# Sparse attention by pairs of heads on halves of the tensor engine, gate products between its steps and z products between those of the state-space mixer

## The chip, the cores and the metric

The kernel runs on one core of a Trainium2 chip. The metric is the time of one execution on the device in microseconds (us), as the median over the runs. The engines are named PE (tensor engine; PEld is its loading of weights), DVE (vector engine), ACT (scalar engine), POOL and SP; each works through its own queue.

## The reference, cut to what matters

The reference is a chain of three transformer blocks over 512 tokens of 1024 features. Only the first block is touched. It runs three mixers on the same normalized input, gates two of them, and joins them in one product:

```
o_nsa = sparse attention: 8 heads of 64 features, 2 groups of keys and values,
        = g0 * attention to compressed keys + g1 * attention to selected blocks + g2 * attention in a window
        (at 512 tokens every block is selected and the window holds every key:
         both are plain causal attention, each with its own keys and values)
o_nsa = o_nsa * silu(gate columns of the input product)
y     = state-space mixer: 8 heads, chunks of 128 tokens
o_ssd = rmsnorm(y * silu(z)) * g_ssd_norm
o_mem = attention to 256 memory tokens, 4 heads of 128
o_mem = o_mem * silu(its gate columns)
x     = rmsnorm(x + [o_nsa, o_ssd, o_mem] @ w_out) * g_final
```

## The kernel before, in words

Activations lie feature-major, as tiles of 128 features by 512 tokens. A float32 product of the large matrices is made as three products of two-part operands (`mm3`, lines 119 to 121, on a `Pair` of a high and a low part). `weight` (from line 96) loads a weight tile through SP and cuts it into parts: the high part is a copy on ACT (line 106), the low part a subtraction on DVE (line 107). There are 12 buffers for parts of 512 columns and 3 for raw tiles. PSUM has 6 banks under the name `ps` (`bank`) and 2 under `pt` (`bank2`).

`linear` goes through the output tiles of a product one at a time. Its first `head` tiles can go k tile by k tile, for 256 tokens and then for the other 256; its last `tail` tiles end by halves too. `Fill` gives out a product in parts of two k tiles (six products), to be put between steps of other work; its `evac` runs behind the last part of a tile.

The first block (`block1`) first does the attention to the memory (`memory`), then the sparse attention (`Nsa.attend`), then the mixer (`ssd`), then the joining product with `w["out"]`. The outputs of the mixers are the twelve tiles `o`: 0 to 3 sparse attention, 4 to 7 mixer, 8 to 11 memory.

`attend` makes queries, keys and values by `linear`, then the compressed scores of all heads, and then goes through 64 units (pair of heads j, head e of the pair, query tile i, branch b). `front` computes a unit's scores: one product over 128 rows (line 206), where the key tile `kp[b, g, e]` is zero in the 64 rows of the other head, plus the causal mask as a product with the identity (line 207); then the maximum on DVE (209, 211), the Exp on ACT (213), and the scaling on DVE (1035, 1036). `back` transposes the probabilities block by block (`turn`, 221), copies them on ACT (223), and multiplies them with the values (1050) into 64 of 128 partitions of a bank; the compressed branch is one more product (1047). Scores are issued three units ahead of their use.

`ssd` makes its inputs by `linear`, then goes through four chunks. Between their steps it calls `fill.run(2)`, 22 parts in all, on the 32 parts of the eight gate products (their evacuation is `ev_g`, lines 912 to 915). What is left is run behind the loop; then the four z products come by `linear` with `ev_z` (1262 to 1264), and then the norm. The joining product takes the parts of all twelve tiles in order of k.

The instructions of an engine are put in order when the kernel is built, by a planner that knows which operands are ready when. In the trace products of a later stage stand among those of an earlier one, as the products of the mixer's inputs do in the last 8 us of the attention.

Of the kernel before, what the change touches and what calls it, by code (L numbers as in the profile page):

```python
# [27 lines left out]
class Pair:  # L28
    """A float32 tensor as two float32r parts whose sum is the tensor."""
# [8 lines left out]
class Core:  # L38
    def __init__(self, ctx, tc):
# [28 lines left out]
                                fill=-1e30, base=0, channel_multiplier=1)  # L68
        self.mean = self.const.tile([P, 1], F32, name="mean")
# [25 lines left out]
    def weight(self, ap):  # L95
        """Parts of a weight tile [P, n], n <= 1024, from DRAM: Pairs of up to 512 columns each."""
# [29 lines left out]
    def split(self, x, g=None, pool=None, tag="xg", into=None, sl=None):  # L126
        """The parts of x * g, g a column per partition."""
# [11 lines left out]

    def linear(self, w, kt, x, evac, head=0, tail=0, pre=None):  # L140
        """F-major product: w [m tiles, P, kt * P] in DRAM, x a Pair per k tile, evac(m, psum, columns).
        The first `head` tiles go k by k, for one half of the tokens and then for the other, so that they can
        start on the first x. The last `tail` tiles end with the first half of the tokens of all of them before
        the second. pre is the norm in front, to be finished behind its squares' products."""
# [4 lines left out]
        for ms in groups:  # L149
# [3 lines left out]
            def mm(m, k, sl):  # L153
# [4 lines left out]
                self.mm3(qs[m][:, sl], ws[m, k // 8][k % 8 // 4][:, o:o + P], x[k][:, sl], k == 0, k == kt - 1)  # L158

            if head and ms[0] == 0:  # L160
                for sl in HALVES:
                    for k in range(kt):
                        for m in ms:
                            mm(m, k, sl)
# [32 lines left out]
    def row_of(self, q, rows, p):  # L197
        """Row p of the tile `rows` on all partitions, into q."""
        self.nc.tensor.matmul(q, self.ident[:, p:p + 1].to_broadcast([P, P]), rows, start=True, stop=True)

    def causal_probs(self, pool, lhs, rhs, i, scale, tag, **kw):
        """exp(s - max) of scale * lhs.T @ rhs for query tile i, keys up to it; and the row sums."""
        nc = self.nc
        n = (i + 1) * P
# [11 lines left out]
    def turn(self, pool, src, n):  # L216
        """The n blocks of src [P, n * P], each transposed: [P, n, P]."""
# [4 lines left out]
        t = pool.tile([P, 4, P], F32, tag="turn", name=self.name("turn"), bufs=3)  # L222
# [3 lines left out]
    def log1p_exp_neg_abs(self, pool, a, tags):  # L226
        """ln(1 + exp(-|a|)) by the series of 2 atanh(u / (2 + u))."""
# [16 lines left out]
    def rsqrt(self, y, q, n, eps, sl=FULL, w=None):  # L244
        """1 / sqrt(q / n + eps) into y, both at columns sl."""
# [17 lines left out]
    def columns(self, row):  # L263
        """A row on all partitions [P, n * P] as token columns [P, n]."""
# [10 lines left out]
class Sums:  # L275
    """Sums over features of tiles that come whole, or by halves of the tokens, in whole [P, 512] tiles.
    `late` takes the last tile straight to the tensor engine; else total() is called for."""
# [6 lines left out]
    def add(self, s, sl):  # L284
        """True when the sum at columns sl is complete, in PSUM."""
# [29 lines left out]
class Norm:  # L315
    """1 / sqrt(mean of squares + eps) per token, as a row on all partitions."""
# [22 lines left out]
class HeadNorm:  # L339
    """1 / sqrt(mean of squares + eps) over each of n tiles of features, for many of them at a time."""  # L340
# [10 lines left out]
    def add(self, h, s):  # L351
        """s, the squares of tile h."""
# [6 lines left out]
    def finish(self, a, b):  # L359
        """Tiles a to b have all been squared."""  # L360
# [3 lines left out]
    def row(self, h):  # L364
        """The row of tile h on all partitions, in PSUM."""
# [7 lines left out]
class Fill:  # L373
    """F-major products given out in small parts, to stand between the steps of other work."""
# [24 lines left out]
    def run(self, n=1):  # L399
        """n parts of two k tiles each, or all of them with n None."""  # L400
# [11 lines left out]
class Pre:  # L412
    """RMS norm in front of a product: parts of x * g, and 1 / rms per token, applied behind it."""
# [22 lines left out]
def post(c, x, y, norm, g, then):  # L436
    """x + y * norm * g in place; `then` gets each tile's number and columns as they are done."""
# [9 lines left out]
def ffn3(c, x, pre, g_post, w_in, w_out, then):  # L447
    """x + rms(swiglu(pre(x)), g_post), x in place."""
# [35 lines left out]
def mlstm(c, x, pre, w_rows, w_v, w_o, w_out, b_i, b_f, head_g, g_post, then):  # L484
    """x + rms(mlstm_mixer(pre(x)), g_post), x in place."""
    nc, mm = c.nc, c.nc.tensor.matmul
    H, L, NC, DK = 4, 128, 4, 128
    with ExitStack() as st:
# [70 lines left out]
        def scores(h):  # L559
            """Weighted scores, queries and keys of head h, and the decays of its state."""  # L560
# [79 lines left out]
def shared_kv(c, pre, w_k, w_v, kd, vd, filler):  # L640
    """Keys, feature-major, and values, token-major, of rms(x) into DRAM."""
# [22 lines left out]
def diff_attention(c, x, pre, w_q, kd, vd, lam_vecs, subln, w_out, lam_init, g_post, then):  # L664
    """x + rms(diff_attention(pre(x)), g_post), x in place."""
    nc, mm = c.nc, c.nc.tensor.matmul
    H, DH = 8, 64
    with ExitStack() as st:
# [38 lines left out]
        def front(j, i):  # L707
            """The difference of the two softmaxes of query tile i."""
# [184 lines left out]
def block1(c, x, w, v, then):  # L893
# [5 lines left out]
    with ExitStack() as out:  # L899
# [18 lines left out]
        for m in range(8):  # L918
            fill.put(w["gates"][m], KD, pre.xg, lambda q, m=m: ev_g(m, q))
# [1029 lines left out]
```

## Time and profile before

| | us |
|---|---|
| median of 3 runs | 3599.95 (3599.71 to 3602.56) |
| span of the profiled execution | 3597.9 |
| PE busy | 3505.6 (97%) |
| PEld busy | 2924.1 (81%) |
| DVE busy | 2058.8 (57%) |
| ACT busy | 1529.4 (43%) |
| POOL busy | 490.8 (14%) |

The runs' time is that of the whole execution on the device, the span runs from the first to the last instruction of one execution under the profiler; the two differ by some 2 us here. A busy share is an average over stages. Matmuls are pipelined and the ends of their records are modelled, so the starts of records tell more than their durations. A plain float32 product is two records, a transposition one. The stages follow each other in the trace like this: sparse attention from its compressed scores, 176 to 305 us; the mixer's inputs to 352, its loop to 405, the rest of the gate products and the z products to 441, the joining product after that.

### The profile page before, as it was taken

What the parts mean: (1) busy time and instruction counts of PE and PEld (TensorE: products, weight loads), DVE (VectorE), ACT (ScalarE), POOL (GpSimd) and SP (SyncE); (2) the same over time, 40 slices, a digit from 0 to 9 for tenths busy, and PEclk for the clock granted to TensorE, in tenths of its full rate; (3) what the DMA queues carried; (4) which work ended last, traced back from release to release, by engine and by line L of the source; (5) the groups of instructions that cost most, each with busy time, mean ns of one, the idle gap of its engine ahead of it and who ended that gap; (6) DMA issues with size and microseconds to landing.
All of it is one profiled execution on the core that took longest, in us unless ns stands there. A gap on an engine that the chain in (4) does not pass through costs nothing. (4 is left out here: it accounts for less than half of the span.)

```text
span 3597.9 us, 48095 instructions
## 1 busy us (share of the span) xinstructions
PE 3505.6 (97%) x18182; PEld 2924.1 (81%) x18182; DVE 2058.8 (57%) x3871; ACT 1529.4 (43%) x2866; POOL 490.8 (14%) x517
## 2 busy tenths in 40 slices
PE   8999999999999999999999999998999999999997
PEld 6767788788788888888887888887888887888886
DVE  6667759995456354633384663439443438673337
ACT  5454544663434242533344543336433335443335
POOL 2100111230010001201110220113110111020112
PEclk9999999999999999999999999999999999999999
DMA  4401232112323333333322133222533223123331
GB/s 146 126 7 48 91 110 94 53 54 71 100 88 98 96 101 96 108 94 100 94 84 70 59 97 103 91 92 74 185 102 103 90 86 92 58 88 94 99 94 65
DMA packets 109712, 323.94 MB, mean 90 GB/s; under 512 B 12328, under 2 KB 28456, under 8 KB 109480
## 3 DMA queue, kind: packets, MB, share of 16 engines
q1 hardware_dynamic: 93648, 299.27, 26.8%
q10 hardware_dynamic: 15832, 21.60, 1.8%
q8 instruction: 143, 2.34, 0.3%
q14 instruction: 89, 0.73, 0.1%
HBM read 308.23 MB, written 12.58 MB: 89 GB/s over the span
## 5 line engine op out<-in xcount | busy, mean ns | idle before, releaser
L119 PE MATMUL ps<-x,hi 128*128 128x512 f32 (+1 forms) x3520 | 1280.9, 366 | 6.0 <-ACT x L136 5.3
L120 PE MATMUL ps<-x,hi 128*128 128x512 f32 (+1 forms) x3520 | 1270.5, 362 | 9.3 <-DVE x L137 8.6
L121 PE MATMUL ps<-x,lo 128*128 128x512 f32 (+1 forms) x3520 | 1265.5, 360 | 2.4 <-DVE lo L107 2.4
L106 ACT CAST hi<-raw 128x512 fp32r<-128x512 f32 (+1 forms) x1112 | 668.9, 612 | 1269.3 <-PE ps L120 1127.3
L107 DVE TENSOR_TENSOR lo<-raw,hi 128x512 fp32r<-128x512 f32 (+1 forms) x1112 | 783.8, 714 | 712.1 <-ACT hi L106 710.2
L120 PEld LDWEIGHTS ps<-x,hi 128*128 128x128 f32 x3520 | 665.8, 189 | 115.7 <-DVE x L137 16.5
L119 PEld LDWEIGHTS ps<-x,hi 128*128 128x128 f32 x3520 | 662.7, 189 | 108.7 <-ACT x L136 9.2
L121 PEld LDWEIGHTS ps<-x,lo 128*128 128x128 f32 x3520 | 665.0, 189 | 103.6 <-DVE lo L107 2.9
L119 PE MATMUL ps<-h,hi 128*128 128x512 f32 (+1 forms) x990 | 367.2, 371 | 0.0
L121 PE MATMUL ps<-h,lo 128*128 128x512 f32 (+1 forms) x990 | 364.4, 368 | 0.0
L120 PE MATMUL ps<-h,hi 128*128 128x512 f32 (+1 forms) x990 | 361.4, 365 | 0.0
L466 POOL TENSOR_TENSOR gt<-gt,gt 128x512 f32<-128x512 f32 x88 | 137.7, 1566 | 1088.9 <-DVE gt L465 941.1
L121 PEld LDWEIGHTS ps<-h,lo 128*128 128x128 f32 x990 | 185.7, 188 | 34.3
L120 PEld LDWEIGHTS ps<-h,hi 128*128 128x128 f32 x990 | 185.8, 188 | 33.4
L119 PEld LDWEIGHTS ps<-h,hi 128*128 128x128 f32 x990 | 186.0, 188 | 30.7
L296 POOL TENSOR_TENSOR sqa<-sqa,sq 128x256 f32<-128x256 f32 (+1 forms) x171 | 166.9, 976 | 303.6 <-ACT sq L326 296.5
L134 DVE TENSOR_TENSOR h<-gt,h 128x512 fp32r<-128x512 f32 x110 | 76.7, 700 | 148.9 <-ACT h L133 146.9
L133 ACT CAST h<-gt 128x512 fp32r<-128x512 f32 x110 | 68.1, 620 | 182.6 <-POOL gt L466 174.4
L465 DVE TENSOR_TENSOR gt<-ps,rbc 128x512 f32<-128x512 f32 x88 | 60.8, 691 | 119.5 <-PE ps L121 119.5
L137 DVE SCALAR_TENSOR_TENSOR x<-x,c,x 128x256 fp32r<-128x256 f32 (+1 forms) x144 | 98.2, 686 | 22.6 <-ACT x L136 22.6
L136 ACT ACTIVATE x<-x,c 128x256 fp32r<-128x256 f32 (+1 forms) x144 | 75.5, 529 | 72.0 <-DVE x L443 56.9
L460 DVE TENSOR_TENSOR gt<-ps,rbc 128x512 f32<-128x512 f32 x88 | 60.8, 690 | 78.6 <-PE ps L121 78.6
(626 smaller groups left out, 4007.1 us busy)
## 6 DMA issues: line engine op xcount, KB each, us to landing
raw<-fi SPq DMA_DIRECT2D x220, 512.0 KB, 3.5
raw<-fo SPq DMA_DIRECT2D x80, 512.0 KB, 3.5
raw<-fo SPq DMA_DIRECT2D x80, 192.0 KB, 2.3
raw<-out SPq DMA_DIRECT2D x16, 512.0 KB, 3.5
raw<-qf SPq DMA_DIRECT2D x16, 512.0 KB, 3.5
raw<-mz SPq DMA_DIRECT2D x16, 512.0 KB, 3.5
raw<-pg SPq DMA_DIRECT2D x16, 512.0 KB, 3.5
raw<-mr SPq DMA_DIRECT2D x9, 512.0 KB, 3.7
```

The source lines that it names most:

```text
L106: nc.scalar.copy(hi[:, :b], raw[:, a:a + b])
L107: nc.vector.tensor_tensor(lo[:, :b], raw[:, a:a + b], hi[:, :b].bitcast(F32), ALU.subtract)
L119: mm(out, lhs.hi, rhs.hi, start=start, stop=False)
L120: mm(out, lhs.hi, rhs.lo, start=False, stop=False)
L121: mm(out, lhs.lo, rhs.hi, start=False, stop=stop)
L133: nc.scalar.copy(hi, x)
L134: nc.vector.tensor_tensor(lo, x, hi.bitcast(F32), ALU.subtract)
L136: nc.scalar.mul(hi, x, g)
L137: nc.vector.scalar_tensor_tensor(lo, x, g, hi.bitcast(F32), ALU.mult, ALU.subtract)
L296: nc.gpsimd.tensor_tensor(self.acc[:, sl], self.part[h][:, sl], s[:, sl], ALU.add)
L460: nc.vector.tensor_tensor(t, q, pre.row, ALU.mult)
L466: nc.gpsimd.tensor_tensor(u, u, hold[0], ALU.mult)
```

## The change

Scores are made for both heads of a pair at once: the key tile holds the same keys in both halves of the rows, and each head's product contracts over its own 64 rows into a bank of its own, in blocks of up to 256 keys that alternate between the halves. The mask is made in the same way, from constants `id2` and `above2`. A unit is now a pair of heads and a query tile, with both branches: 16 units, one ahead. Their value products alternate between the halves of the output partitions. A unit calls `fill.run(1)` twice; the fill holds seven of the eight gate products. The eighth and the four z products are given out in the mixer's loop; the multiplication with z follows behind the loop. The joining product starts with a head of four tiles, in the order of k 0 to 3, 8 to 11, 4 to 7.

```diff
+        self.id2 = self.const.tile([P, 2, P], BF, name="id2")
+        self.above2 = self.const.tile([P, 2, P], BF, name="above2")
+        for src, dst in ((self.identb, self.id2), (self.above, self.above2)):
+            for r in range(2):
+                for h in range(2):
+                    nc.vector.tensor_copy(dst[64 * r:64 * r + 64, h], src[64 * h:64 * h + 64])
...
-    def linear(self, w, kt, x, evac, head=0, tail=0, pre=None):
+    def linear(self, w, kt, x, evac, head=0, tail=0, pre=None, order=None):
...
+            ks = order if first and order else range(kt)
...
-    def causal_probs(self, pool, lhs, rhs, i, scale, tag, **kw):
+    def pair_scores(self, lhs, rhs, i):
+        mm, n = self.nc.tensor.matmul, (i + 1) * P
+        qs, rows = [self.bank(), self.bank()], [slice(0, 64), slice(64, 128)]
+        for a in range(0, n, 256):
+            b = min(a + 256, n)
+            for q, r in zip(qs, rows):
+                mm(q[:, a:b], lhs[r, i * P:n], rhs[r, a:b], start=a == 0, stop=False)
+        for h in range(2):
+            for q, r in zip(qs, rows):
+                mm(q[:, i * P:n], self.id2[r, h], self.above2[r, h], start=False, stop=h == 1)
+        return qs
+
+    def probs(self, pool, q, n, scale, tag, **kw):
-        q = self.bank()
-        nc.tensor.matmul(q[:, 0:n], lhs, rhs[:, 0:n], start=True, stop=False)
-        nc.tensor.matmul(q[:, i * P:n], self.identb, self.above, start=False, stop=True)
...
-            nsa.attend(st, o, place)
...
+            fill = Fill(c)
+            gate = lambda m: fill.put(w["gates"][m], KD, pre.xg, lambda q: ev_g(m, q))
+            for m in (4, 5, 6, 7, 0, 1, 2):
+                gate(m)
+            nsa.attend(st, o, place, fill)
+            gate(3)
...
-        fill = Fill(c)
-        for m in range(8):
-            fill.put(w["gates"][m], KD, pre.xg, lambda q, m=m: ev_g(m, q))
...
-        c.linear(w["out"], 12, og, ev_o, tail=2)
+        c.linear(w["out"], 12, og, ev_o, head=4, tail=2, order=[0, 1, 2, 3, 8, 9, 10, 11, 4, 5, 6, 7])
...
-        kp = {(b, g, e): til(f"kp{b}{g}{e}", pool=ap) for b in range(2) for g in range(2) for e in range(2)}
-        for (b, g, e), t in kp.items():
-            nc.gpsimd.memset(t[64 * (1 - e):64 * (1 - e) + 64], 0.0)
+        kp = {(b, g): til(f"kp{b}{g}", pool=ap) for b in range(2) for g in range(2)}
...
-        def front(j, e, i, b):
+        def front(j, i):
+            n, ex = (i + 1) * P, {}
+            for b in range(2):
+                for e, q in enumerate(c.pair_scores(qT[j], kp[b, j // 2], i)):
+                    x, sm = c.probs(a2, q, n, SC, "e", bufs=8)
+                    rs = til("rs_", (P, 1), pool=a2, bufs=8)
+                    nc.vector.reciprocal(rs, sm)
+                    nc.vector.tensor_scalar(x[:, 0:n], x[:, 0:n], rs, gv[:, i, 2 * j + e, b + 1:b + 2], ALU.mult, ALU.mult)
+                    ex[b, e] = x
             return ex
...
-        def back(j, e, i, b, ex):
+        def back(j, i, ex):
+            g, n, pt = j // 2, (i + 1) * P, {}
+            if i == 0:
                 oq[0] = c.bank()
+            for b in range(2):
+                for e in range(2):
+                    pt[b, e] = c.turn(a2, ex[b, e], i + 1, bufs=6)
+                fill.run(1)
+            dst = [oq[0][64 * e:64 * e + 64, i * P:n] for e in range(2)]
+            for e in range(2):
+                mm(dst[e], vcp[:, 2 * j + e], pc[g][:, i * P:n], start=True, stop=False)
+            for b in range(2):
+                for t in range(i + 1):
+                    for e in range(2):
+                        mm(dst[e], vt[b][:, t, 64 * g:64 * g + 64], pt[b, e][:, t], start=False, stop=b == 1 and t == i)
...
+        units = [(j, i) for j in range(4) for i in range(4)]
+        ready = [front(*units[0])]
         for n, u in enumerate(units):
+            if n + 1 < len(units):
+                ready.append(front(*units[n + 1]))
             back(*u, ready.pop(0))
...
+        zs = [None] * 4
+
+        def ev_z(m, q):
+            zs[m] = til(f"z{m}")
+            nc.vector.tensor_tensor(zs[m], q, r, ALU.mult)
+            nc.scalar.activation(zs[m], zs[m], AF.Silu)
+
+        for m in range(4):
+            fill.put(w["z"][m], KD, pre.xg, lambda q, m=m: ev_z(m, q))
...
         fill.run(None)
         norm = Norm(c, 4)
...
+        for m in range(4):
+            nc.vector.tensor_tensor(o[m], o[m], zs[m], ALU.mult)
             norm.square(o[m])
-
-        c.linear(w["z"], KD, pre.xg, ev_z)
```

The attention of the third block (`diff_attention`), which called `causal_probs` too, makes the same products in place and then calls `probs`.

## Rows read from the trace of the kernel before

**Rows 1.** Windows: core, stretch, its length, busy time and count per engine, clock, DMA.

```profile
190.00:297.00 107.00, 106.38 (x669) 70.09 (x669) 64.77 (x241) 58.71 (x183) 0.00 (x0) 1.00 0.02 6
352.00:405.50 53.50, 53.38 (x344) 42.21 (x342) 44.19 (x108) 33.43 (x51) 6.47 (x5) 1.00 0.18 55
```

**Rows 2.** Tensor engine groups by form, 190 to 297 us: busy, mean ns, idle before.

```profile
L1050 PE MATMUL ps<-turn,vt 128*64 128x128 f32 x292 | 40.8, 280 | 0.3 <-ACT turn L223 0.2
...
L221 PE MATMUL pt<-ident,e 128*128 128x128 f32 x146 | 27.0, 287 | 0.2 <-ACT pc L1029 0.2
...
L206 PE MATMUL ps<-kp,q 128*128 128x512 f32 x28 | 14.5, 599 | 0.0
...
L1047 PE MATMUL ps<-pc,vcp 128*64 128x128 f32 x60 | 12.5, 290 | 0.0
```

**Rows 3.** Timeline, tensor engine: start, from first start to last end, trains of eight records.

```profile
198.74 1.09 PE L221 MATMUL pt<-ident,e 128*128 128x128 f32 x8
...
281.02 1.09 PE L1050 MATMUL ps<-turn,vt 128*64 128x128 f32 x8
...
356.40 0.66 PE L1225 MATMUL ps<-M,xdt 128*64 128x128 f32 x8
```

**Rows 4.** Timeline, tensor engine: score steps of four lengths, one after the other.

```profile
180.75 0.44 PE L206 MATMUL ps<-kp,q 128*128 128x128 f32 x2
181.03 0.22 PE L207 MATMUL ps<-above,identb 128*128 128x128 bf16 x1
181.09 0.65 PE L206 MATMUL ps<-kp,q 128*128 128x256 f32 x2
...
181.63 0.65 PE L206 MATMUL ps<-kp,q 128*128 128x256 f32 x2
...
186.02 0.86 PE L206 MATMUL ps<-kp,q 128*128 128x384 f32 x2
...
186.78 1.08 PE L206 MATMUL ps<-kp,q 128*128 128x512 f32 x2
...
187.75 1.08 PE L206 MATMUL ps<-kp,q 128*128 128x512 f32 x2
```

**Rows 5.** Timeline: the mixer's last products, the first splits, the mixer's norm.

```profile
401.64 0.40 PE L120 MATMUL ps<-x,hi 128*128 128x512 f32 x1
...
403.04 0.40 PE L120 MATMUL ps<-x,hi 128*128 128x512 f32 x1
...
405.10 0.38 PE L1227 MATMUL ps<-cx,sn 128*64 128x128 f32 x2
...
406.56 0.68 DVE L912 TENSOR_TENSOR gt<-ps,rbc 128x512 f32<-128x512 f32 x1
...
406.68 1.14 ACT L133 CAST s<-o 128x512 fp32r<-128x512 f32 x2
...
444.71 1.13 PE L301 MATMUL pt<-sq,ones 128*128 128x512 f32 x2
...
452.11 1.29 ACT L133 CAST x<-o 128x512 fp32r<-128x512 f32 x2 [1.31 <-DVE o L1269]
```

**Rows 6.** Scalar engine groups by line, 352 to 405.5 us.

```profile
L913 ACT ACT_TABLE_LOAD x5 | 6.4, 1283 | 0.1
...
L913 ACT ACTIVATE gt<-gt 128x512 f32<-128x512 f32 x5 | 3.2, 631 | 0.1
```

**Rows 7.** Timeline, tensor engine: products of 256 columns, the 1st and 25th of a run.

```profile
492.86 0.28 PE L119 MATMUL ps<-x,hi 128*128 128x256 f32 x1
...
495.74 0.29 PE L119 MATMUL ps<-s,hi 128*128 128x256 f32 x1
```

**Rows 8.** Timeline and windows (granted clock behind POOL): an idle, and the clock after it.

```profile
33.00 1.02 PE L269 MATMUL pt<-mean,rbc 128*128 128x1 f32 x4 [5.76 <-DVE rbc L254]
...
32.00:34.00 2.00, 1.00 (x5) 1.00 (x5) 2.00 (x2) 0.44 (x1) 1.92 (x2) 0.50 0.44 178
34.00:36.00 2.00, 2.00 (x6) 1.61 (x6) 1.34 (x3) 1.28 (x3) 0.06 (x1) 0.50 0.00 0
```

More of the change, by code (lines that the diff above doesn't have):

```diff
@@ L157, in mm @@
                 o = (k % 4) * P
-                self.mm3(qs[m][:, sl], ws[m, k // 8][k % 8 // 4][:, o:o + P], x[k][:, sl], k == 0, k == kt - 1)
-            if head and ms[0] == 0:
+                self.mm3(qs[m][:, sl], ws[m, k // 8][k % 8 // 4][:, o:o + P], x[k][:, sl], k == 0, k == ks[-1])
+            first = head and ms[0] == 0
+            ks = order if first and order else range(kt)
+            if first:
                 for sl in HALVES:
-                    for k in range(kt):
+                    for k in ks:
                         for m in ms:
@@ L214, in causal_probs, with turn @@
         return e, mx[:, 1:2]
-    def turn(self, pool, src, n):
+    def turn(self, pool, src, n, bufs=3):
         nc = self.nc
@@ L221, in turn @@
             nc.tensor.transpose(q[:, k * P:(k + 1) * P], src[:, k * P:(k + 1) * P], self.ident)
-        t = pool.tile([P, 4, P], F32, tag="turn", name=self.name("turn"), bufs=3)
+        t = pool.tile([P, 4, P], F32, tag="turn", name=self.name("turn"), bufs=bufs)
         nc.scalar.copy(t[:, 0:n], q[:, 0:n * P].rearrange("p (a b) -> p a b", b=P))
@@ L713, in front @@
             n = (i + 1) * P
-            es = [c.causal_probs(d2, qT[j][:, i * P:n], kv[j][0][b], i, 1.0, f"e{b}") for b in range(2)]
+            es = []
+            for b in range(2):
+                q = c.bank()
+                mm(q[:, 0:n], qT[j][:, i * P:n], kv[j][0][b][:, 0:n], start=True, stop=False)
+                mm(q[:, i * P:n], c.identb, c.above, start=False, stop=True)
+                es.append(c.probs(d2, q, n, 1.0, f"e{b}"))
             rs = til("rs", (P, 2), pool=d2)
@@ L905, in block1, with ev_g @@
                 memory(c, cst, pre, w, v, o, place, nsa)
-            nsa.attend(st, o, place)
-        op = out.enter_context(c.tc.tile_pool(name=c.name("o"), bufs=1))
-        r = pre.row
-        def ev_g(m, q):
-            t = c.t512("gt")
-            nc.vector.tensor_tensor(t, q, r, ALU.mult)
-            nc.scalar.activation(t, t, AF.Silu)
-            i = m if m < 4 else m + 4
-            nc.gpsimd.tensor_tensor(o[i], o[i], t, ALU.mult)
-        fill = Fill(c)
-        for m in range(8):
-            fill.put(w["gates"][m], KD, pre.xg, lambda q, m=m: ev_g(m, q))
+            r = pre.row
+            def ev_g(m, q):
+                t = c.t512("gt")
+                nc.vector.tensor_tensor(t, q, r, ALU.mult)
+                nc.scalar.activation(t, t, AF.Silu)
+                i = m if m < 4 else m + 4
+                nc.gpsimd.tensor_tensor(o[i], o[i], t, ALU.mult)
+            fill = Fill(c)
[4 more added lines that the diff above has]
+            gate(3)
+        op = out.enter_context(c.tc.tile_pool(name=c.name("o"), bufs=1))
         ssd(c, pre, r, w, v, o, op, fill)
@@ L970, in rope, with attend @@
         nc.gpsimd.tensor_tensor(dst, src, t, ALU.add)
-    def attend(self, st, o, place):
+    def attend(self, st, o, place, fill):
         c, nc, til, v = self.c, self.c.nc, self.til, self.v
@@ L1037, in front @@
             return ex
         oq = [None]
-        def back(j, e, i, b, ex):
-            h, g, n = 2 * j + e, j // 2, (i + 1) * P
-            if e + i + b == 0:
+        def back(j, i, ex):
+            g, n, pt = j // 2, (i + 1) * P, {}
+            if i == 0:
                 oq[0] = c.bank()
-            dst = oq[0][64 * e:64 * e + 64, i * P:n]
-            if b == 0:
-                mm(dst, vcp[:, h], pc[g][:, i * P:n], start=True, stop=False)
-            pt = c.turn(a2, ex, i + 1)
-            for t in range(i + 1):
-                mm(dst, vt[b][:, t, 64 * g:64 * g + 64], pt[:, t], start=False, stop=b == 1 and t == i)
-            if (e, i, b) == (1, 3, 1):
+            for b in range(2):
[5 more added lines that the diff above has]
+                mm(dst[e], vcp[:, 2 * j + e], pc[g][:, i * P:n], start=True, stop=False)
+            for b in range(2):
+                for t in range(i + 1):
+                    for e in range(2):
+                        mm(dst[e], vt[b][:, t, 64 * g:64 * g + 64], pt[b, e][:, t], start=False, stop=b == 1 and t == i)
+            if i == 3:
@@ L1258, in ssd @@
         norm = Norm(c, 4)
-        def ev_z(m, q, sl):
-            t = c.t512("gt")
-            nc.vector.tensor_tensor(t, q, r, ALU.mult)
-            nc.scalar.activation(t, t, AF.Silu)
-            nc.vector.tensor_tensor(o[m], o[m], t, ALU.mult)
+        for m in range(4):
+            nc.vector.tensor_tensor(o[m], o[m], zs[m], ALU.mult)
             norm.square(o[m])
-        c.linear(w["z"], KD, pre.xg, ev_z)
         for i in range(4):
```

12 lines of the change are left out of this document (1 added, 11 removed).

## The prediction, made before the changed kernel was run

> **What bounds the kernel now.** I read the stages by windows first, then the groups of instructions in the attention stage, then the order of time on the tensor engine around each product that the change touches. The profiled execution spans 3597.9 us; the median of the runs is 3599.95, so what the sum gives is taken off the median as it stands (the two differ by 2 us, which is in the range). The tensor engine bounds the stage that is changed: between 190 and 297 us, which hold some 60 of the 64 steps of the sparse attention, it is busy 106.38 of 107.0 us while the vector engine has 64.77 and the scalar engine 58.71 [rows 1]. The mixer's loop is as dense: 53.38 of 53.5 us [rows 1]. So moving products cannot fill idle time, for there is next to none. The change can gain only where the same arithmetic takes the tensor engine less time, and it loses wherever moved products were the cover for a wait.
>
> **Products of values on column halves.** A value product writes 64 of the 128 output partitions. Before, the steps of one head follow each other on one half: a train of 8 records runs 1.09 us, and with 0.28 us for the last [rows 2] the starts lie (1.09 - 0.28) / 7 = 0.116 us apart [rows 3]. The mixer's products already alternate the halves: the same 8 records of the same shape run 0.66 us, so starts lie (0.66 - 0.287) / 7 = 0.053 us apart [rows 3], with 0.287 us taken for the last one here. The trace thus shows that two halves run at once in this very form. Attention has 64 steps, with 320 records of values and 64 of compressed values; of the 384, rows 2 show 352 in their stretch. They go from 384 x 0.116 = 44.5 to 384 x 0.053 = 20.4 us, plus a lead-in of 0.06 in each of 16 trains: **gain 23 us** (20 to 24).
>
> **Scores on row halves.** Before, a score product contracts over 128 rows of which 64 are zero. From one start to the next, mask included, a step takes 0.34 us for 128 keys, 0.54 for 256, 0.76 for 384 and 0.97 for 512 [rows 4], 2.61 together, times 16 = 41.8 us. Two heads on the two row halves would be 21 if they overlap fully, 42 if not at all; no row of this trace has two row halves at work. What speaks against the full half is the weights: keys are cut into blocks of 256, each with its own two loads per head. That makes 2 branches x 2 heads x 2 records x (1+1+2+2) blocks = 48 records for each pair of heads, 192 in all. The transposes carry a load of 128 columns per record and follow at (1.09 - 0.287) / 7 = 0.115 us [rows 2, 3]; if loads go one at a time at that pace, 192 x 0.116 = 22.3 us. The mask doubles from 64 to 128 products of 64 rows; the step from a mask to the next product is 0.06 us [rows 4], so 128 take 7.7 alone and 3.8 in pairs. I take the pairs, as the value halves do pair: 22.3 + 3.8 = 26, **gain 15 us**. Bounds: 21 (all overlaps) and minus 4 (nothing overlaps, masks doubled).
>
> The Trainium skill bears on this place alone ("TensorE: Matmul & The Clock Gate", Part 3, Packing small matmuls): products on different row groups run concurrently, four of 32 rows at 3.07 times the speed. No row here shows it; by it the term would lie near 21. Its section on LDWEIGHTS says that loading takes time by columns, not rows, which speaks against the change here: half the rows do not halve a load; no load of half the rows is in this trace either.
>
> **Changes of shape.** In the stretch of rows 2, 352 half-width records at 0.116 are 40.8 us, 146 transposes at the same pace 16.9, and 56 score steps (14 of each length) 14 x 2.61 = 36.5: 94.3 of 107.0. The other 12.7 us, 13.5 for all 64 steps, go with the change between half-width and full-width products, about twice a step, 0.1 us each. Afterwards there are 16 groups with three shapes, 48 to 64 changes if the planner keeps a group's products together: 5 to 7 us. **Gain 7 us** (0, if the planner mixes shapes as it does now, to 9).
>
> **Gate products moved into the attention.** 28 parts of six products; six follow each other in 1.40 us [rows 5], so some 39 us of tensor work leave the mixer and enter attention, in sum nothing. With them come 14 weight casts on each of the two other engines, 7 evacuations and 7 Silu. The scalar engine must swap its table between Exp and Silu: 1.283 us a load, 0.631 for the Silu [rows 6]. A gate tile can thus hold up the copies of transposes, for which only two banks exist, by 2 x 1.28 + 0.63 = 3.2 us; 7 times that is 22 us if nothing covers it, 0 if the 2.8 us of parts per group and the probabilities a group ahead do. Vector engine: 64.77 x 64 / 60 = 69, plus 21 operations of 0.68 [rows 5] and the compressed part, 90 us; scalar about 63 + 9 + 22 = 94; the tensor engine has about 115 to 120. It stays the bound, so I take a quarter: **loss 6 us**. The dropped memsets are on an engine that idles here.
>
> **The mixer and its end.** The loop has 22 places for parts and now 20 parts (one gate tile, four z). The last wait, from the second group's decays to its output products, is covered now by products such as those from 401.64 on; without them I count the two places lost, 2.8 us, and a product or two of other cover: **4 us** (0 to 6). Behind the last output product, at 405.10 + 0.38, the vector engine adds up the outputs, and the first output is split only then: its high part starts at 406.68 and takes 0.57, the low part is a vector pass over one tile, 0.68 [rows 5]. Before, the remaining gates and z products hid that; now none is left. Bounds are 1.8 us (high part only) and 5 (four z multiplications of 0.68 go ahead of the low part); I take **4 us**. The order 0 to 3, 8 to 11, 4 to 7 then gives 8 tiles x 4 x 3 products of 256 columns, 24 in 2.88 us [rows 7] or 11.5 us, as cover for the norm of the mixer, which takes 7.4 us from its sum to the next split [rows 5] and four multiplications and squares before it, about 12: **1 us** late. After an idle of 5.76 us up to 33.0 the granted clock was 0.50, the lower of the two levels, 1.2 GHz, up to 36 at least [rows 8]: of 3 to 4 us of products half is lost, **2 us** (0 if both gaps stay short). Halving the columns in the head costs 288 x (0.120 - 0.117) = 1 [rows 5, 7], with its weights **1.5 us**. The weights of four tiles need 12 of 12 buffers, but eight are free before the z products end. The eight small copies at the start fall before the first load lands: 0.
>
> **Sum.** 23 + 15 + 7 - 6 - 4 - 4 - 1 - 2 - 1.5 = 26.5 us off 3599.95: **3573 us**.
>
> **The rivals.**
> *Row halves do not overlap* (loads or the array serialise them). Score steps cost what they did and masks 4 us more: 19 us dearer than the sum, 3592. For it: no such pair is in the trace, and the loads are close to the stream. Against it: the column halves pair in just this way. 0.17.
> *Attention is paced by the softmax chain*, the one that ends slower. A group's four scores, the outputs' bank and the gate's bank fill all six banks, so the next group's scores may not start beside this group's products. Per group the vector engine has 4 x 64.77 / 60 = 4.3 us, and a further 1 us of scalar work before the first transpose; the two parts cover 2.8. That is 2.5 us idle, 16 times 40 instead of 6: 3607. It decides from 33 us of idle on, 2.1 us a group. Against it: 60 steps now wait 0.6 us in all [rows 1], and a bank of scores is free once the Exp has read it. 0.12.
> *No wait at all*: the planner covers attention and the join, and 17 us of losses vanish: 3556. Nothing now waits, which speaks for it; the missing parts at the end speak against it. 0.08.
> *The sum*: 0.63, with its own range of 3562 to 3586 from the bounds of shapes, waits and scores.
>
> **Numbers.** A difference under 0.2%, 7 us, is no change here. The sum, the last rival and 0.09 of the first lie below 3592.8: faster 0.80. The rest of the first and 0.02 of the chain's lie within: same 0.10. The rest of the chain's is slower, 0.10. The range 3558 to 3597 leaves out the chain's case and part of the no-wait case.
>
> **What would show it.** Right: trains of value products at 0.05 to 0.06 us a record; score records of two row halves overlapping, below 0.7 us per pair for 256 keys; attention with its 28 parts about 125 us long; tensor idle of some 8 us around the end of the mixer's loop with the clock down after it. Wrong: score starts of the second head only after the first's end; the tensor engine waiting for copies of transposes or for probabilities in each group; more than 100 changes of shape; the head of the output product waiting for weights.

## The result, and the profile after

The changed kernel takes 3582.44 us (median of four runs, 3581.4 to 3585.29), the kernel before 3599.83 beside it; the ratio is 0.995, 95% interval 0.9938 to 0.9962. That is 17.4 us off where 26.5 were forecast: inside the range and inside the likeliest case's own range, on its slow side. The profiled execution spans 3583.5 us, 14.4 less than before; it was the longest of the four runs (3585.29), so the stretches below account for 14.4 and not for 17.4.

To see where the time went, the table cuts the span at five landmarks of the tensor engine or its evacuations, read from the first and last start of a line: the first product of the compressed scores, the first decay product of the mixer's loop, the last evacuation of the join (its copy out of PSUM), and the first and last product of the levels in the second block's recurrence, which the change does not touch.

| us | before | after |
|---|---|---|
| up to the compressed scores | 176.5 | 178.0 |
| attention and the mixer's input products | 171.6 | 175.3, with 28 gate parts more |
| mixer's loop, its end, join | 163.8 | 139.1, with 28 gate parts less |
| from the join to the second block's levels | 103.3 | 103.3 |
| second block's levels | 217.1 | 221.9 |
| rest of the span | 2765.6 | 2765.9 |

With 1.40 us a part [rows 5] the 28 parts are 39.2 us of tensor work. The attention thus gained 171.6 + 39.2 - 175.3 = 35.5 us, the mixer and the join lost 139.1 + 39.2 - 163.8 = 14.5, the second block lost 4.8, and 1.5 was lost ahead of the change (a second profile of the same kernel, below, comes there at 176.0).

The windows of the changed kernel, with the columns of [rows 1]: a stretch of the attention, then the mixer's end.

```profile
200.00:300.00 100.00, 98.28 (x855) 74.62 (x854) 69.21 (x230) 73.66 (x189) 8.78 (x7) 1.00 0.12 36
400.00:410.00 10.00, 5.70 (x48) 4.70 (x46) 8.12 (x18) 7.45 (x11) 0.00 (x0) 0.93 0.57 160
410.00:420.00 10.00, 3.25 (x7) 1.45 (x5) 6.17 (x12) 5.73 (x9) 2.85 (x2) 0.50 0.16 63
420.00:430.00 10.00, 10.00 (x75) 9.48 (x75) 7.22 (x11) 3.37 (x6) 0.00 (x0) 0.89 0.22 68
```

The attention is still dense on the tensor engine, with gate products in it and a busier scalar engine. The mixer's end is not: between 400 and 420 the tensor engine works 9 of 20 us, and the second ten stand at a granted clock of 0.50, the lower level, 1.2 GHz.

The tensor engine's timeline of the changed kernel in the attention (start, from first start to last end): scores of a pair of heads for 512 and 256 keys, and a train of value products. They answer to [rows 3, 4].

```profile
204.47 1.14 PE L218 MATMUL ps<-kp,q 64*128 64x256 f32 x8
205.43 0.28 PE L221 MATMUL ps<-above,id 64*128 64x128 bf16 x4
205.54 1.09 PE L218 MATMUL ps<-kp,q 64*128 64x256 f32 x8
...
222.29 0.65 PE L218 MATMUL ps<-kp,q 64*128 64x256 f32 x4
222.78 0.28 PE L221 MATMUL ps<-above,id 64*128 64x128 bf16 x4
...
250.53 0.44 PE L1080 MATMUL ps<-pc,vcp 128*64 128x128 f32 x4
250.80 1.92 PE L1084 MATMUL ps<-turn,vt 128*64 128x128 f32 x32
252.65 0.70 PE L218 MATMUL ps<-kp,q 64*128 64x256 f32 x4
```

Both heads' scores for 512 keys run from 204.47 to the masks at 205.43, 0.96 us, and with the masks to 205.54, 1.07; one head alone took 0.97 with its mask before [rows 4]. In the train of 32, starts lie (1.92 - 0.27) / 31 = 0.053 us apart, as the mixer's did [rows 3].

The timeline of the mixer's end in the changed kernel, all engines:

```profile
403.16 1.28 ACT L1224 ACT_TABLE_LOAD   x1
...
403.29 0.38 PE L1270 MATMUL ps<-cx,sn 128*64 128x128 f32 x2
...
404.45 0.63 ACT L1224 ACTIVATE z<-z 128x512 f32<-128x512 f32 x1
405.10 1.28 ACT L1256 ACT_TABLE_LOAD   x1
...
407.80 0.43 PE L1268 MATMUL ps<-M,xdt 128*64 128x128 f32 x2 [4.13 <-DVE M L1257]
...
409.62 0.63 PE L1270 MATMUL ps<-cx,sn 128*64 128x128 f32 x2
410.29 1.12 DVE L1272 SCALAR_TENSOR_TENSOR o<-xbc,c,ps 128x128 f32<-128x128 f32 x4 [1.94 <-PE ps L1270]
411.33 2.49 DVE L1303 TENSOR_TENSOR o<-o,z 128x512 f32<-128x512 f32 x4
412.05 1.24 ACT L345 ACTIVATE sq<-o 128x512 f32<-128x512 f32 x2 [4.54 <-DVE o L1303]
...
414.97 1.15 ACT L345 ACTIVATE sq<-o 128x512 f32<-128x512 f32 x2 [1.69 <-POOL sqa L315]
...
416.03 2.16 ACT L139 CAST s<-o 128x512 fp32r<-128x512 f32 x4
...
417.00 2.08 PE L328 MATMUL pt<-sqa,ones 128*128 128x512 f32 x2 [6.75 <-POOL sqa L315]
...
418.87 1.91 PE L320 MATMUL pt<-sq,ones 128*128 128x512 f32 x2
...
419.80 1.20 PE L125 MATMUL ps<-s,hi 128*128 128x256 f32 x1
```

The tensor engine waits 4.13 us for the second group's decays; ahead of their Exp the scalar engine has a Silu of z with a table load on either side, 403.16 to 406.38. The outputs' products end at 410.2. The first split of a sparse-attention output (L139) then stands behind the multiplications by z and all four squares, at 416.03, and in the tensor engine's queue the norm's total (L328) and its last square (L320) stand ahead of the join's first product, which starts 9.6 us after that end and at half rate.

### The profile page after: what moved, and what is told of

The parts are those of the page before. It is cut to its first block, busy times and chain, and to the rows that moved or that the text cites. A ratio compares the mean times of both kernels' runs of the same rounds, so it can differ in the third digit from the quotient of the medians.

```text
span 3583.5 us, 48642 instructions
## 1 busy us (share of the span) xinstructions
PE 3483.7 (97%) x18454; PEld 2924.8 (82%) x18454; DVE 2055.7 (57%) x3879; ACT 1539.3 (43%) x2879; POOL 485.6 (14%) x509
## 3 DMA queue, kind: packets, MB, share of 16 engines
q1 hardware_dynamic: 93648, 299.27, 26.5%
## 5 line engine op out<-in xcount | busy, mean ns | idle before, releaser
L126 PEld LDWEIGHTS ps<-x,hi 128*128 128x128 f32 x3552 | 674.8, 190 | 113.2 <-DVE x L143 16.3
L125 PEld LDWEIGHTS ps<-x,hi 128*128 128x128 f32 x3552 | 671.5, 190 | 107.6 <-ACT x L142 9.2
L127 PEld LDWEIGHTS ps<-x,lo 128*128 128x128 f32 x3552 | 673.6, 190 | 101.8 <-issue 2.5
L139 ACT CAST h<-gt 128x512 fp32r<-128x512 f32 x110 | 68.1, 620 | 182.6 <-POOL gt L485 174.4
L142 ACT ACTIVATE x<-x,c 128x256 fp32r<-128x256 f32 (+1 forms) x144 | 75.4, 528 | 72.4 <-DVE x L462 57.3
```

Source lines behind the costliest of these rows:

```text
L125: mm(out, lhs.hi, rhs.hi, start=start, stop=False)
L126: mm(out, lhs.hi, rhs.lo, start=False, stop=False)
L127: mm(out, lhs.lo, rhs.hi, start=False, stop=stop)
L139: nc.scalar.copy(hi, x)
L142: nc.scalar.mul(hi, x, g)
```

## The experiments

Each kernel is the changed one with the edit shown; its time is put as the ratio to the kernel before, run on the same chip. The changed kernel stands at 0.995; 0.001 is 3.6 us. "Attention", "mixer and join" and "levels" are the stretches of the table above.

**The two packings, undone one at a time and together.**

```diff
 e1: for e in range(2): compressed product of head e; for b: for t: mm(dst[e], ...)      # was: b, t, then e
 e2: qs, rows = [self.bank(), self.bank()], [slice(0, 64), slice(0, 64)]                  # was: 0..64, 64..128
```

> The changed kernel with one edit: the value products of a group of the sparse attention go through all of one head and then all of the other, so that neighbours in the tensor engine's queue write the same half of the columns. Work and count of products are the same. Theory (the halves of the columns pair, and the tensor engine sets the pace of the attention): 384 records go back from about 0.053 to 0.116 us apart, 24 us less a little for the seams, so the changed kernel's 3582 becomes 3603, and the trains of value products show 0.11 to 0.12 us a record. Rival (the attention is now paced by another engine, so tensor time in it is partly free): under 10 us longer, below 3592.

> The changed kernel with one edit: the scores and masks of both heads of a pair are taken from the same half of the rows (the first one), so no two row halves can be at work; the count, size and order of products are the same. The second head of each pair gets the first head's scores, so the output is not the reference's. Theory (row halves overlap): a pair of 512 keys goes from 0.96 us for 8 records to about 8 x 0.22 = 1.76, one of 128 from 0.22 to 0.44, 2.0 us for the four lengths, with masks 2.3; times 2 branches and 4 pairs of heads, 18 us longer: 3600. Rival (the weight loads or the array let row halves overlap little, and the attention's gain came from elsewhere): under 6 us longer, below 3588.

> Both packings undone in the changed kernel at once (value products one head after the other, and scores of both heads from the same half of the rows, so that the second head has the first one's scores and the output is not the reference's); what is left of the change are the moved products, the larger groups and the order of the join. Theory (the terms add up, and the moves by themselves only cost): 3582 + 21 + 18 = 3621, some 20 us slower than the kernel before. Rival (the two terms use the same slack, or the moves gain by themselves): 3605 or less.

Values undone: 0.9988 (0.9979 to 0.9997), attention 189.6 us, 14.3 more. Rows undone: 0.9986 (0.9977 to 0.9994), attention 189.0, 13.7 more. Both: 1.0029 (1.0019 to 1.004), attention 203.4, 28.1 more. The terms add up to 0.1 us, the mixer and the join stay within 0.7 us, so both packings are real and on the path; each costs less to undo than the experiment expected. What is left of the change without them is slower than the kernel before, as expected, by 10 us and not 20; 4.8 of them lie in the levels. The timeline of the run with the values undone, a group of 512 keys, and of the run with the rows undone, a pair of heads at 512 keys:

```profile
255.22 0.43 PE L1080 MATMUL ps<-pc,vcp 128*64 128x128 f32 x2
255.49 1.58 PE L1083 MATMUL ps<-turn,vt 128*64 128x128 f32 x13
256.80 0.32 PE L1080 MATMUL ps<-pc,vcp 128*64 128x128 f32 x1
256.91 0.27 PE L1083 MATMUL ps<-turn,vt 128*64 128x128 f32 x1
256.96 0.27 PE L1080 MATMUL ps<-pc,vcp 128*64 128x128 f32 x1
257.01 1.97 PE L1083 MATMUL ps<-turn,vt 128*64 128x128 f32 x18
258.91 0.70 PE L218 MATMUL ps<-kp,q 64*128 64x256 f32 x4
```

```profile
237.00 1.99 PE L218 MATMUL ps<-kp,q 64*128 64x256 f32 x8
238.83 0.38 PE L221 MATMUL ps<-above,id 64*128 64x128 bf16 x4
```

The 36 records of values take 258.91 - 255.22 = 3.69 us, 0.102 each, against 252.65 - 250.53 = 2.12, 0.059 each, in the changed kernel. This edit does not undo the packing in full: where the first head's train ends, from 256.80 on, the second head's products already run between its records, on the other half. On one half alone the starts lie (256.91 - 255.49) / 13 = 0.109 us apart. So the 14.3 us are less than the alternation gives over whole trains on one half. The pair of scores takes 1.83 us against 0.96: 1.9 times. Part of what the rows cost is hidden, too: with them undone the tensor engine idles 1.1 us in the stretch where the changed kernel idles 4.3.

**Packing alone**, with gates, z products and join as before.

```diff
-            nsa.attend(st, o, place, fill)
+            nsa.attend(st, o, place, Fill(c))     # empty; gates, z and the join as in the kernel before
```

> Packing alone: the sparse attention of the changed kernel, with no gate products between its steps; gates, z products and the joining product as in the kernel before. Theory (the terms of packing stand by themselves): 23 + 15 + 7 = 45 us off the kernel before, and the mixer's end keeps its cover: 3555. Rival (without the gate products the tensor engine waits in each group for probabilities and copies of transposes, so that the moved products are what makes the packing pay): 16 groups lose 1 to 2 us each, 16 to 32 us, and the time is 3570 to 3587, with idle of the tensor engine before the transposes and the value products.

0.9957 (0.9944 to 0.9971), the same as the whole change within the intervals. That equality owes something to the levels, 216.7 us here against 221.9: over attention, mixer and join, the stretches that the change touches, packing alone takes 155.7 + 163.7 = 319.4 us, the whole change 314.4, the kernel before 335.4. The rival's time holds: the attention takes 155.7 us where the changed kernel's, without its 39.2 us of gate parts, takes 136.1, so it loses 19.6 by their absence, although it has no table swaps for gates. The rival's reason, waits in each group, holds in small part only. Its timeline at 233 us:

```profile
232.82 0.44 PE L1078 MATMUL ps<-pc,vcp 128*64 128x128 f32 x4
233.19 0.61 PE L218 MATMUL ps<-kp,q 64*128 64x128 f32 x4
234.36 0.93 PE L240 MATMUL pt<-ident,e 128*128 128x128 f32 x6 [0.56 <-ACT turn L242]
235.22 1.09 PE L1082 MATMUL ps<-turn,vt 128*64 128x128 f32 x14
...
237.25 0.87 PE L1082 MATMUL ps<-turn,vt 128*64 128x128 f32 x10 [0.34 <-ACT turn L242]
```

Transposes and values wait for copies of transposes, but the recorded waits of the attention sum to 5.2 us against 4.0 in the changed kernel. The clock counts for more. Between 190 and 200 us, in the kernel before, the changed one and this one (the granted clock stands behind POOL):

```profile
190.00:200.00 10.00, 9.48 (x66) 7.38 (x67) 7.28 (x30) 6.60 (x25) 0.00 (x0) 1.00 0.18 52
190.00:200.00 10.00, 10.00 (x61) 7.00 (x61) 7.03 (x28) 4.50 (x18) 0.00 (x0) 0.82 0.00 0
190.00:200.00 10.00, 9.36 (x37) 5.05 (x36) 4.67 (x21) 4.43 (x18) 0.00 (x0) 0.50 0.00 0
```

By the traces' clock records it stands at the lower level from 185.7 to 206.2, 20.5 us, here and for 6.8 us in the changed kernel: up to 6.8 us lost more. Idle is 1.4 more (5.7 against 4.3). The rest, some 11 us, goes with shorter trains: the same products stand in 131 stretches of one shape (transposes, scores or values; a gate part between them ends one) in place of 96. That the cuts cost it is argued, not shown.

**The join's order.**

```diff
-  order=[0, 1, 2, 3, 8, 9, 10, 11, 4, 5, 6, 7])
+  order=[8, 9, 10, 11, 0, 1, 2, 3, 4, 5, 6, 7])
```

> The changed kernel with one edit: the head of the joining product starts with the memory's tiles 8 to 11, whose parts are ready before the mixer ends, and then takes 0 to 3. Theory (the join is late because its first operands, tiles 0 to 3, are split only behind the mixer's squares, and the norm's total stands ahead of it): 48 products of 256 columns at 0.117 us can follow the mixer's last output at 410, so of the 9.6 us from there to the join's first product, and the 2.3 us at half rate, some 6 go; the norm's chain, 15.6 us from the last output to the first part of tile 4, then sets the pace: 3576. Rival (the norm's chain is the path anyway): less than 2 us, 3581 to 3583.

The start flags of the sums follow the order. 0.9926 (0.9914 to 0.9939), 8.6 us less, but only part of it is the theory's: mixer and join take 133.8 us, 5.3 less where some 6 were expected. Products of tiles 8 to 11 now stand in the last wait of the loop too, which is gone. The norm's total, which stands behind 48 of the head's products in the queue, still waits 6.09 us. The levels took 217.0 us in this run, 4.9 less, and the attention 0.9 more.

**One gate tile back to the mixer; parts at the attention's start.**

```diff
 e5: for m in (4, 5, 6, 7, 0, 1): gate(m) ... nsa.attend(...); gate(2); gate(3)
 e6: ready = [front(*units[0])]; fill.run(3)
```

> The changed kernel with one edit: the gate tile 2 goes from the attention to the mixer, 24 parts in each. Theory (the mixer's end lacks cover: its last wait is 4.1 us and nothing is left to run in it): two parts of 1.4 us stand in that wait and two behind it, 4 to 5 us shorter less 1 us for a group or two of the attention without parts: 3578. Rival (the attention needs those parts as much, about 1.1 us for each group without them, and the mixer's wait is not filled by what stands in the queue): 3582 to 3585.

> The changed kernel with one edit: three gate parts are called for behind the first group's scores, ahead of the second's, and are missing at the end of the attention. Theory (the start of the attention loses 3.7 us of waits and 2 us at the lower clock, which the prediction left out): 3 to 4 us shorter, less 1 us at the end: 3580. Rival (the planner had these parts at hand there already and does not use them, or the end loses as much): 3582 to 3584.

Neither gains: 0.9953 (0.9941 to 0.9966) and 0.9962 (0.9948 to 0.9975). With the gate tile in the mixer the loop's last wait is filled, though the join then waits 4.9 us for its first split and 3.5 for the norm's total, and mixer and join take 141.6 us, 2.5 more with 5.6 us of work more; but the attention, with 5.6 us of work less, is only 2.9 shorter. What one stage gains in cover the other loses. Three parts at the start lengthen attention and input products by 3.9 us, and the levels were 3.1 shorter.

**The table swaps of the scalar engine.**

```diff
-                nc.scalar.activation(t, t, AF.Silu)       # gates, and the same for z
+                nc.scalar.activation(t, t, AF.Exp)
```

> The changed kernel with Exp in place of Silu for the gates and z, so that the scalar engine does not swap tables for them in the attention and the mixer's loop; the gated outputs are not the reference's. Theory (the swaps are hidden in the attention, and only the last one in the mixer is on the path): the attention from the compressed scores to the last values stays within 1 us of 133.8, the mixer's last wait shrinks from 4.1 by two table loads of 1.28: 3579 to 3580. Rival (the term of the prediction, a quarter of 22 us in the attention): attention 6 us shorter, 3574 or less.

0.9925 (0.9912 to 0.9937). The experiment's theory falls and the prediction's term holds: the attention takes 169.6 us, 5.7 less. The last wait shrinks from 4.1 to 2.6.

**More cover for the join, and a gate function without swaps.**

```diff
-                for sl in HALVES:
-                    for k in ks:
+                for part, sl in [(p, s) for p in (ks[:4], ks[4:8], ks[8:]) for s in HALVES]:
+                    for k in part:                         # order as above: 8..11, 0..3, 4..7
...
 silu as x / (1 + exp(-x)):    Exp, + 1, reciprocal, product
 silu as h (1 + tanh h), h = x / 2:    Tanh, one vector pass
```

> The run with the join's new order, and further: the head of four tiles goes through memory's tiles 8 to 11 for both halves of the tokens, then 0 to 3 for both, then the mixer's 4 to 7, so that up to 192 products of 256 columns (22 us) can stand before the first that needs the mixer's norm. Theory (what is left at the mixer's end, 6.1 us of the tensor engine waiting for the norm's squares and some 2 us at half rate behind it, is missing cover and nothing else): some 46 products, 5.4 us, now stand between the mixer's last output and the norm's total; the wait falls to about 1 us and the time from 3574 to 3567 to 3569. Rival (the chain of multiplications, squares and splits sets the join's end): 3573 to 3575.

> As the run with more cover, and the Silu of the gates and of z written as x / (1 + exp(-x)): Exp on the scalar engine, so that no tables are swapped in the attention and the mixer's loop, then an addition and a reciprocal on the vector engine and a second multiplication on POOL; the output is the reference's. Theory (the swaps held up the attention by 5 to 6 us, and neither the vector engine, 60 to 65 of 100 us busy there, nor POOL is near the path): 5 to 6 us less than the run with more cover, 3561 to 3564. Rival (two more vector passes for each gate and z hold up the probabilities as much as the swaps did): no gain, 3566 to 3570.

> As the run with more cover, and the Silu of the gates and of z written as h (1 + tanh h) with h = x / 2: Tanh on the scalar engine, one more vector pass of 0.69 us for each tile, no reciprocal; the output is the reference's. The Trainium skill ("ScalarE: Activation LUTs", Table sets) has Exp and Tanh in one set; no run so far shows a Tanh. Theory (the swaps of tables held up the attention by 5 to 6 us, as the run with Exp in place of Silu showed, and it was the reciprocals of 3.35 us on the vector engine that cost the other form its 34 us): the loads of 1.28 us before and behind each gate's function are gone from the attention, which is 5 us shorter; 3567 becomes 3561 to 3563. Rival (Tanh needs a load of its own too, or the extra vector pass holds up the probabilities): 3567 to 3570.

More cover: 3567.11 us, 0.9904 (0.989 to 0.9917), as its theory said. Mixer and join take 126.8 us, 12.3 less than in the changed kernel, and the total's wait is 1.57:

```profile
416.72 1.13 PE L330 MATMUL pt<-sqa,ones 128*128 128x512 f32 x2 [1.57 <-POOL sqa L317]
```

With the reciprocals the kernel is back at 0.9999 (0.999 to 1.0008): attention 194.6 us, mixer and join 144.8. The groups of the vector engine between 200 and 300 us show the likely cause:

```profile
L941 DVE RECIPROCAL gt<-gt 128x512 f32<-128x512 f32 x6 | 20.1, 3348 | 0.1
```

Each fills the vector engine, which makes the probabilities, for 3.35 us; up to the loop the tensor engine now waits 7.1 us for copies of transposes, 5.8 for banks that Exp reads and 1.7 for the vector engine. The run does not separate the reciprocals from the addition (0.43 us) and the second product on POOL that came with them.

With Tanh: 0.9894 (0.9878 to 0.991), 3565.53 us, attention 169.5 us, 5.9 less than with Silu, mixer and join 127.2; the interval overlaps that of the run with Silu, so the gain over it rests on the stretch. The Trainium skill ("ScalarE: Activation LUTs", Table sets) puts Exp and Tanh in one set; the groups of the scalar engine from 180 to 312 us agree: the changed kernel's seven loads before a gate's function and seven behind it, then what is left of them in the run with Tanh, a single load for the mixer's inputs.

```profile
L935 ACT ACT_TABLE_LOAD x7 | 9.0, 1283 | 0.1
L232 ACT ACT_TABLE_LOAD x7 | 9.0, 1283 | 9.9 <-DVE e L230 9.9
```

```profile
L938 ACT ACTIVATE gt<-gt 128x512 f32<-128x512 f32 x7 | 4.4, 630 | 2.7 <-DVE gt L936 2.7
...
L1216 ACT ACT_TABLE_LOAD x1 | 1.3, 1283 | 0.0
```

Both the run with more cover and the one with Tanh beat both kernels.

**The changed kernel once more**, for the second block.

> The changed kernel as it is, once more, beside the two others. Theory (the 4.8 us that the second block loses between its first and last level products, 221.9 against 217.1 us with the same waits, belong to the change): 3582 again, and 221 to 222 us in that stretch. Rival (they are chance of one profiled execution): 217 us in that stretch, and a median up to 5 us lower.

3582.44 us, 0.9946 (0.9933 to 0.9958), and the levels took 222.1 us: the loss comes again with the same kernel. What is different there is the clock. The products there stand in the same order in both kernels. After the same wait for squares the timeline of the changed kernel, then that of the kernel before:

```profile
666.53 1.05 PE L375 MATMUL pt<-ones,sq 128*128 128x1 f32 x8 [0.92 <-ACT sq L367]
667.44 1.45 PE L1662 MATMUL ps<-e 128*128 128x64 f32 x8
668.65 0.77 PE L125 MATMUL ps<-x,hi 128*128 128x512 f32 x1
```

```profile
685.32 1.05 PE L356 MATMUL pt<-ones,sq 128*128 128x1 f32 x8 [0.93 <-ACT sq L348]
686.24 1.08 PE L1625 MATMUL ps<-e 128*128 128x64 f32 x8
687.13 0.48 PE L119 MATMUL ps<-x,hi 128*128 128x512 f32 x1
```

The eight level products take 1.45 us in the one and 1.08 in the other. Over the stretch, windows give a granted clock of 0.94 and 0.96:

```profile
595.70:817.60 221.90, 209.34 (x1213) 183.45 (x1212) 201.52 (x383) 131.49 (x195) 59.89 (x65) 0.94 0.16 50
```

```profile
615.20:832.30 217.10, 203.91 (x1214) 178.96 (x1213) 201.78 (x383) 130.97 (x195) 59.66 (x64) 0.96 0.17 51
```

The time without work is 13 us in both, within 0.7; the busy time is 5.4 longer. By the clock records the tensor engine stands at the lower level for 27.2 us of the stretch in the changed kernel and for 17.0 in the kernel before; half of the difference is 5.1 us, which is the loss.

## Why the prediction was right, and where it was off

To set the terms against the traces, the table counts each product of the tensor engine from its start to the next one's start, idle left out, in the stretch of attention and input products. A change of shape is thus booked to the product ahead of it. "Swaps gone" is the run with Exp in place of Silu.

| us | before | changed | values undone | rows undone | packing alone | swaps gone |
|---|---|---|---|---|---|---|
| value products | 50.2 | 26.5 | 40.9 | 26.3 | 33.7 | 24.9 |
| scores and masks | 45.9 | 30.5 | 30.8 | 49.8 | 39.6 | 27.8 |
| transposes | 22.8 | 20.8 | 20.7 | 19.7 | 27.6 | 19.7 |
| gate parts, input products | 44.7 | 88.6 | 88.6 | 87.5 | 44.4 | 89.8 |
| compressed scores, small ones | 4.6 | 4.7 | 4.8 | 4.8 | 4.8 | 4.8 |
| idle | 3.5 | 4.3 | 4.0 | 1.1 | 5.7 | 2.7 |

- **Value products: right.** 23 us were forecast, 50.2 - 26.5 = 23.7 came. Undoing them costs less (14.3) because the larger groups stay and the halves still meet where trains meet. The pace was read a little high: 0.116 holds the wider first step of a train of eight, and on one half the records go at 0.109.
- **Scores on row halves: right.** 15 forecast, 45.9 - 30.5 = 15.4 came (18.1 with the swaps gone). The Trainium skill ("TensorE: Matmul & The Clock Gate", Part 3, Packing small matmuls) agrees that row groups run at once; the 21 worked out by it was too much. What kept it from 21, the loads or the doubled masks, no run separates.
- **Changes of shape: counted too low, and in part twice.** 7 us were forecast; what is left beside the two rows above is 2.0 on the transposes. The seams of values and scores are booked in their rows, and the first step of each train was in the 0.116 already. By a count on the timelines the stretches of one shape fell from 210 to 96 (gate products end a stretch and are not counted), where 48 to 64 changes were forecast to remain; with the stretches of gate and input products it is 125, over the 100 that the prediction named as a sign of being wrong. The three terms together: 45 forecast, 41.1 came, and 118.9 - 72.4 = 46.5 with the swaps gone. So what is missing here is the swaps' doing, which the prediction had as a term of its own.
- **Gate products in the attention: the size right, in part by choice.** 6 were forecast, 5.7 is what the swaps cost. The quarter of 22 us was not worked out, so that it fits is partly luck. Little of it is idle (4.3 against 2.7 us): with the swaps gone the first three rows take 72.4 us in place of 77.8, in 80 stretches in place of 96. "In sum nothing" for the parts themselves fails both ways. They are dearer there: the row of gate parts and input products grew by 43.9 us where 39.2 were counted, part of it at the lower clock, and this is what the attention lacks of its forecast. And they are cover: without them the attention loses 19.6 us, or 25.3 against the run with no swaps. The rival of the softmax chain did not come: the recorded waits of the stretch sum to 4.0 us, and to 5.2 without the parts, far from 33.
- **The mixer's end: the sum was right, the places in part wrong.** 4 + 4 + 1 + 2 + 1.5 = 12.5 us were forecast, 14.5 measured: 10 more without work (139.1 - 126.94 against 163.8 - 161.64) and 4.5 at the lower clock and in the join's halved products. The last wait is 4.1, as said, but not for missing cover alone: 1.5 of it goes with the table swaps, which the prediction counted in the attention only. And the step "the first output is split only then", 1.8 to 5 us, had the join start behind one split; in the queue it stands behind the norm's total, 9.6 us after the outputs. That the sum came out is partly luck.
- **Second block: not in the sum.** 4.8 us at the lower clock, with the same waits.
- **The start of the attention: not in the sum.** The idle of 1.54 us at 183 is no loss of the change, for the kernel before has one of 1.51 us there. But the clock, 1.00 before, is 0.84 from 180 to 190 and 0.82 from 190 to 200: up to 3.4 us, within the rows of the table. Three parts put there did not win it back.

The prediction's sign of an attention of about 125 us with its parts did not follow from its sum: from the first compressed score to the last copy of an output the kernel before takes 129.2 us, and 129.2 - 39 + 39.2 = 129.4; the changed kernel takes 133.8.

In sum the forecast of the attention was 39 and 35.5 came, of the end 12.5 and 14.5; with 4.8 in the second block and 1.5 ahead of the change that is 14.7 by the landmarks, the span shows 14.4, and the medians 17.4.

## What to carry to other kernels

Two halves of the tensor engine do run at once, for columns (0.053 us a record against 0.109 on one half) and for rows (0.96 us a pair against 1.83). The packed products keep their gain only while something else keeps trains whole and the clock up: in its stretches packing alone won 16.0 us of the whole change's 21.0, and with gates that need no table swaps the attention won 5.7 more. An experiment that undoes a packing shows that it is real, but its price need not be the term of the sum: set the term against the kernel before as well. When cover is moved, list what stands in the queue at the place it leaves, the small products of norms included, and order the next stage by which operands are ready first; that one line took 5.3 us off the mixer's end and the join, and going through the ready tiles for both halves of the tokens 7.0 more. A function from another table set, or reciprocals over whole tiles, can cost what queues behind them: 5.7 us for 14 loads, and over 30 us for twelve reciprocals with the two passes that came beside each, in stages where neither engine was the bound.

## What the runs showed of the hardware that was not expected

- A reciprocal of 128 x 512 on the vector engine takes 3.35 us, a pass with an addition 0.43.
- The levels of the second block, with the same products in the same order and 12.5 to 13.2 us without work in every profile, took 217.1, 216.7 and 217.0 us (before, packing alone, new order), 218.8 (parts at the start, more cover), 220.2 (Tanh), and 221.7 to 222.1 in the eight other profiles, two of them of the same kernel. The granted clock accounts for it: by the clock records the lower level, 1.2 GHz, lasted 17.0 us of the stretch in the first three, 20.4, 23.8 and 27.2 in the others, in this order. What decides it is not settled: the stage starts at another time in each of them, and no run varied that alone.
